# First norm by scaling and transposing, with the loads of tokens and weights in another order, in a one-core hybrid encoder layer

## The chip, the cores and the metric

The kernel runs on one core of a Trainium2 chip. The metric is the device time of one execution in microseconds; the median of the runs is what counts. The engines of the core are TensorE (PE in the profile; its weight loads are PEld), VectorE (DVE), ScalarE (ACT), GpSimd (POOL) and SyncE (SP, which here only issues DMAs).

## What is computed

One layer of an encoder on 512 tokens of 1024 channels, in float32. The first step is an RMS norm; its result `h` goes through one wide projection whose columns feed a recurrent branch (RG-LRU), a gated DeltaNet branch in both directions, and gates. Both branches are projected, gated, added to the tokens; a second norm and a SwiGLU feed-forward follow, then a last norm.

```python
def rmsnorm(x, g):
    y = x * rsqrt(mean(x * x, -1) + EPS)
    return y * g

h = rmsnorm(x, mix_norm)                     # the step that is changed
rx, ry, qkv, z, ba, gates = split(h @ w_in)  # 1024 x 9248
y_rnn = rglru_branch(rx, ry, ...) @ w_rnn_proj
y_dn = deltanet_branch(qkv, z, ba, ...) @ w_dn_proj
x = x + (sigmoid(g_rnn) * y_rnn + sigmoid(g_dn) * y_dn) @ w_out
gt, up = split(rmsnorm(x, ffn_norm) @ w_gate_up)
x = x + (silu(gt) * up) @ w_down
return rmsnorm(x, final_norm)
```

## The kernel before

Nearly all arithmetic is matrix products on TensorE. A float32 operand is split into a high part (rounded to the format fp32r) and a low part (the rest), and a product is the sum of three: high by high, high by low, low by high (`mm3`, L591). A split costs one copy on ScalarE and one subtraction on VectorE.

**The first norm.** Tokens come as four blocks of 128 (`xs`, L505 to L511), each 128 x 1024 with tokens on the partitions. For each block `rms_rstd` (L463) sums the squares, on ScalarE for the first block of a pair and on VectorE for the second, and takes the reciprocal of the root. The projection needs channels on the partitions, so a block has to be transposed. `norm_scale` (L485) multiplies a 128 x 128 identity by the tokens' factors, which gives a diagonal matrix `dg`, and `norm_transpose` (L490) multiplies each 128 x 128 piece of the tokens with it on TensorE: scaling and transposing are one float32 product. Four such products (two pieces of channels, two blocks of tokens) fill one PSUM buffer of the three called `ax`. ScalarE then writes the high part `hh` with the gain as a scale, VectorE the low part `hl` (L502, L503).

**The projection.** A step of the projection takes 128 columns of `w_in`. `weights` (L588, by `stage`, L571) loads them into one of three buffers `wraw` and splits them into `whi` and `wlo`, two buffers each; `in_proj` (L600) multiplies them with `hh` and `hl`, eight pieces of channels, 24 products with 512 tokens. For the first four calls in the program the tokens are taken as two halves of 256 (L604), so 48 products with 256 columns. `rg_front` (L686) is such a step for one of the twelve blocks of the recurrent branch, followed by a convolution and four small gate products, whose weights are loaded to the one buffer `graw` in two DMAs (L692, L693). A narrow step (L620 to L634) projects the 32 columns of `ba`. The second norm (L1230 on) already scales the tokens on VectorE and then transposes the scaled ones with `turn` (L441), TensorE's transpose against the identity.

**The order of the work.** Nothing is issued as it is written. `Rec` (L319) notes every operation with an estimated cost, and `Plan.order` (L144) lays them out: it steps through time, and whenever an engine is free it takes that operation, among those whose inputs are done and whose buffers are free, which has the lowest key. The key is the stage's entry in the table `TIMES` (L35) plus the offset `plan.t` inside the stage; `spend` (L433) begins a new stage. Stages beyond the table (the feed-forward and the end) follow in the order of the program. Costs per engine are in L340 to L372; `TABLES` (L58) says which function tables serve which function of ScalarE, so that the planner can count the loads. SyncE's DMAs are laid out by the same keys. The loads of tokens have the offset -300 (two blocks) and -20 (the other two), weights -40.

In the order before, SyncE issues the four token blocks, then the columns of `ba`, the weights of one step, gate weights, and more weights. TensorE begins with the products on `dg`, and among them runs the `ba` step and then the step of recurrent block 5 with 512 tokens.

Of the kernel before, what the change touches and what calls it, by code (L numbers as in the profile page):

```python
# [53 lines left out]
class Plan:  # L54
# [3 lines left out]
    TABLES = {AF.Exp: ("exp", "lnexp"), AF.Tanh: ("exp", "sigmoid", "silu", "gelu"), AF.Sigmoid: ("sigmoid",), AF.Sqrt: ("sqrt",),  # L58
              AF.Ln: ("lnexp",), AF.Silu: ("silu",), AF.Gelu_apprx_tanh: ("gelu",)}
# [259 lines left out]
class Rec:  # L319
# [5 lines left out]
    def __getattr__(self, op):  # L325
        real = getattr(self.real, op)

        def call(*a, **kw):
# [25 lines left out]
            elif e == "ACT":  # L354
                cost = (51 if psum else 93) + 0.834 * n + 93 * (ptr if n > 1 else len(ins) - 1) + (93 if len(outs) > 1 else 0)
                if op == "activation":
                    table = Plan.TABLES.get(a[2])
# [13 lines left out]
            else:  # L371
                cost = {"tensor_tensor": 150 + 2.1 * n, "memset": 35 + 0.834 * n, "affine_select": 140 + 0.886 * n}.get(op, 240 + 0.84 * n)  # L372
# [6 lines left out]
def trunk(ctx: ExitStack, tc: tile.TileContext, x, mix_norm, w_in, rg_conv_w, rg_conv_b, rg_wa, rg_ba, rg_wx, rg_bx,  # L379
# [42 lines left out]
    def small(shape, tag, bufs=2, dt=F32):  # L422
        return new(sp, shape, tag, bufs, dt)
# [39 lines left out]
    def rms_rstd(src, c):  # L463
        ssq = small([P, 1], "ssq", 4)
        if c % 2:
# [40 lines left out]
    for c in range(NT):  # L506
# [3 lines left out]
        if c == 1:  # L510
            plan.t = -20.0  # L511
# [1064 lines left out]
```

## Time and profile before

| | |
|---|---|
| median of 3 runs | 1075.23 us (1075.0 to 1075.24) |
| the profiled execution | 1074.94 us |
| its span, from the first to the last instruction | 1073.2 us |
| mean granted TensorE clock | 0.998 |
| PE busy | 1052.4 us, 6793 matmuls |
| VectorE busy | 905.1 us |
| ScalarE busy | 665.2 us, of it 67 table loads, 86.0 us |
| DMA | 118.59 MB, mean 111 GB/s |

How to read the rows below: a row of the timeline is start, length (us), engine, line, operation, what is written and read, how many were merged, and in brackets the idle time before it and what ended it. All operations are issued through one helper, so that all have the line L373; one goes by the names of the buffers. A row of groups ends with busy time, mean ns of one, and idle time before. A row of windows begins with the stretch, its length, and then busy time and number of instructions for PE, PEld, DVE, ACT and POOL, the clock, the DMA share and GB/s. A busy PE includes the drain of matmuls that overlap, so that the length of one matmul (0.28 to 0.4 us) is more than the distance to the next.

### The profile page before, as it was taken

The numbers are of one execution on the slowest core, as the hardware profiler recorded it, in microseconds if no ns is written. First come the engines' busy times: TensorE is split into PE (matmuls) and PEld (weight loads), VectorE is DVE, ScalarE is ACT, GpSimd is POOL, SyncE is SP. The second block draws the span as 40 slices with busy tenths as digits, with TensorE's granted clock in tenths as the row PEclk, the third lists the DMA queues.
The fourth block names the chain that finished last, engine by engine and source line by source line (L and its number), as shares of the span: only waits on it lengthen the run. The fifth ranks groups of instructions, "written<-read, shape, count | busy, mean of one in ns | idle before, by whom it ended". The sixth has DMA issues, their size and how long they took to land.

```text
span 1073.2 us, 17710 instructions
## 1 busy us (share of the span) xinstructions
PE 1052.4 (98%) x6793; PEld 915.9 (85%) x6793; DVE 905.1 (84%) x1631; ACT 665.2 (62%) x1191; POOL 44.0 (4%) x93
## 2 busy tenths in 40 slices
PE   7999999999999999999999999999999999999997
PEld 6988887888878887988898888889999999998885
DVE  6669999778986996699669947669999988889997
ACT  6899899795457437655784445357454544446664
POOL 2000000003010101101010000000000000000000
PEclk9999999999999999999999999999999999999999
DMA  7332423223231132122312214455567433425633
GB/s 202 103 89 57 131 79 89 70 74 103 84 90 50 45 108 60 41 79 76 82 40 70 79 47 143 132 181 177 178 218 259 142 99 99 118 80 196 212 135 104
DMA packets 165892, 118.59 MB, mean 111 GB/s; under 512 B 5680, under 2 KB 152224, under 8 KB 165808
## 3 DMA queue, kind: packets, MB, share of 16 engines
q1 hardware_dynamic: 164336, 114.18, 35.6%
q10 hardware_dynamic: 1184, 3.15, 0.8%
q8 instruction: 53, 0.87, 0.3%
q14 instruction: 31, 0.25, 0.1%
q0 software_dynamic: 288, 0.13, 0.1%
HBM read 109.59 MB, written 7.86 MB: 109 GB/s over the span
## 4 chain that ended last, share of the span: by engine, by line
PE 84%; DVE 7%; ACT 5%; DMA 1%; issue 1%; SPq 0%; DVEq 0%; ACTq 0%
PE mm L373 48%; PE ax L373 23%; PE st L373 14%; DVE t L373 5%; ACT t L373 3%; DVE wlo L373 1%; ACT na L373 1%; ACT whi L373 1%; DMA wraw<-in_w_in_dram 1%; DVE na L373 1%; ACT L373 1%; DMA wraw<-in_w_gate_up_dram 0%; ACT ax L373 0%; SPq L373 0%; ACT hh L373 0%
## 5 line engine op out<-in xcount | busy, mean ns | idle before, releaser
L373 DVE TENSOR_TENSOR t<-t,t 128x512 fp32r<-128x512 f32 (+20 forms) x466 | 246.9, 544 | 21.8 <-ACT t L373 14.5
L373 PE MATMUL mm<-hl,whi 128*128 128x512 f32 (+2 forms) x704 | 242.5, 356 | 0.4 <-DVE hl L373 0.4
L373 PE MATMUL mm<-hh,whi 128*128 128x512 f32 (+2 forms) x704 | 241.9, 356 | 0.7 <-ACT whi L373 0.7
L373 ACT CAST whi<-wraw 128x1024 fp32r<-128x1024 f32 (+3 forms) x142 | 133.1, 940 | 161.0 <-PE mm L373 78.1
L373 DVE TENSOR_TENSOR wlo<-wraw,whi 128x1024 fp32r<-128x1024 f32 (+3 forms) x141 | 153.2, 1089 | 58.0 <-ACT whi L373 22.1
L373 PE MATMUL mm<-hh,wlo 128*128 128x512 f32 (+1 forms) x688 | 152.3, 355 | 0.0
L373 PEld LDWEIGHTS mm<-hh,whi 128*128 128x128 f32 (+1 forms) x704 | 132.4, 188 | 18.5 <-ACT whi L373 1.5
L373 PEld LDWEIGHTS mm<-hl,whi 128*128 128x128 f32 (+1 forms) x704 | 132.5, 188 | 18.0 <-DVE hl L373 1.5
L373 PE MATMUL ax<-t,t 32*32 32x32 f32 (+3 forms) x1062 | 139.9, 286 | 3.0 <-ACT t L373 2.8
L373 PEld LDWEIGHTS mm<-hh,wlo 128*128 128x128 f32 x688 | 116.2, 189 | 17.4
L373 PEld LDWEIGHTS ax<-t,t 128*128 128x128 f32 (+1 forms) x1062 | 108.7, 159 | 21.0 <-ACT t L373 6.9
L373 ACT CAST t<-t 128x512 fp32r<-128x512 f32 (+2 forms) x128 | 81.5, 652 | 55.2 <-DVE t L373 50.3
L373 PE MATMUL mm<-t,t 128*128 128x256 f32 (+1 forms) x468 | 90.6, 336 | 0.6 <-DVE t L373 0.6
L373 ACT ACT_TABLE_LOAD x67 | 86.0, 1283 | 4.4 <-PEq L1562 1.7
L373 DVE SCALAR_TENSOR_TENSOR t<-mm,par,t 128x511 f32<-128x511 f32 (+1 forms) x108 | 79.5, 743 | 3.4 <-ACT t L373 2.7
L373 PE MATMUL mm<-t,whi 128*128 128x512 f32 x320 | 82.2, 394 | 0.0
L373 PEld LDWEIGHTS mm<-t,t 128*128 128x128 f32 x468 | 72.7, 190 | 9.6 <-DVE t L373 0.8
L373 PEld LDWEIGHTS mm<-t,whi 128*128 128x128 f32 x320 | 59.2, 188 | 12.1 <-ACT whi L373 0.2
L373 ACT ACTIVATE t<-t 128x128 f32<-128x128 f32 (+4 forms) x84 | 46.1, 559 | 18.9 <-DVE t L373 16.8
L373 ACT CAST t<-wraw 128x1024 fp32r<-128x1024 f32 (+1 forms) x48 | 41.7, 870 | 21.0 <-DMA wraw<-in_w_gate_up_dram 8.3
L373 DVE TENSOR_TENSOR t<-wraw,t 128x1024 fp32r<-128x1024 f32 (+1 forms) x48 | 47.9, 998 | 2.3 <-ACT t L373 2.2
L373 PE MATMUL mm<-t,wlo 128*128 128x512 f32 x160 | 44.6, 396 | 0.0
(212 smaller groups left out, 1672.3 us busy)
## 6 DMA issues: line engine op xcount, KB each, us to landing
wraw<-in_w_in_dram SPq DMA_DIRECT2D x72, 512.0 KB, 3.8
wraw<-in_w_gate_up_dram SPq DMA_DIRECT2D x44, 512.0 KB, 4.1
wraw<-in_w_rnn_proj_dram SPq DMA_DIRECT2D x16, 384.0 KB, 3.5
bg<-in_w_down_dram SPq DMA_DIRECT2D x11, 512.0 KB, 4.6
sums<-bg SPq DMA_DIRECT2D x11, 512.0 KB, 4.7
wraw<-sums SPq DMA_DIRECT2D x11, 512.0 KB, 4.5
wraw<-in_w_down_dram SPq DMA_DIRECT2D x22, 256.0 KB, 2.7
wraw<-in_w_down_dram SPq DMA_DIRECT2D x11, 512.0 KB, 3.6
```

The costliest lines, as they stand in the source:

```text
L373: self.plan.add(e, lambda: real(*a, **kw), outs, ins, cost, tail, table)
```

## The change

1. `norm_scale` and `dg` go. `norm_transpose` scales each block on VectorE into a new 128 x 1024 buffer and transposes the scaled pieces with `turn`.
2. The sum of squares: for the first block of each pair ScalarE takes 512 channels and VectorE the other 512, whose scaled sum enters the root as its bias; for the second block ScalarE takes all 1024.
3. The first pair of token blocks is loaded and normed in one stage, the second pair in a stage of its own, parameters and `ba` in two more. By the keys, SyncE's order becomes: token blocks 0 and 1, the weights of recurrent block 0, its gate weights, the weights of recurrent block 1, token blocks 2 and 3, and then the other weights.
4. Twenty products of the matrix of ones with itself are put ahead of the norm on TensorE; their result is not used.
5. The first three projection steps (recurrent blocks 0, 1, 2) take `weights_k`, which splits into buffers of the large pool (22 buffers) instead of `whi` and `wlo`. `weights_k` and `parts_of` are the same functions as before, moved up from the feed-forward.
6. The gate weights of the first three blocks are loaded with the offset -12 instead of -40.
7. The planner: Exp and Ln no longer share a table, strided copies on ScalarE cost 100 ns more, GpSimd's operations have another price.
8. `TIMES` has new values for all stages up to the second norm (159 entries for 156), so that the order changes there on all engines. In the new table the first steps are recurrent blocks 0 and 1, then block 2, `ba`, and blocks 5, 4 and 3.

The core of the diff, without the numbers of the table:

```diff
-    TABLES = {AF.Exp: ("exp", "lnexp"), ...
-              AF.Ln: ("lnexp",), ...
+    TABLES = {AF.Exp: ("exp",), ...
+              AF.Ln: ("ln",), ...
...
+                if op == "copy" and len(dims) > 2 and dims[-1][1] <= 64:
+                    cost += 100
...
-                cost = {"tensor_tensor": 150 + 2.1 * n, ...}.get(op, 240 + 0.84 * n)
+                cost = {...}.get(op, 240 + 1.2 * n)
...
+    def rms_rstd(src, halves):
+        sa, rst, rin = (small([P, 1], t, 4) for t in ("ssq", "rst", "rin"))
+        n = 512 if halves else D
+        A.activation(four(shape=(P, D))[:, 0:n], src[:, 0:n], AF.Square, accum_out=sa)
+        bias = eps_t
+        if halves:
+            bias = small([P, 1], "ssh", 4)
+            V.scalar_tensor_tensor(two(), src[:, n:D], 1.0, src[:, n:D], ALU.mult, ALU.mult, accum_out=bias)
+            V.tensor_scalar(bias, bias, 1.0 / D, EPS, ALU.mult, ALU.add)
+        act(rst, sa, AF.Sqrt, scale=1.0 / D, bias=bias)
         V.reciprocal(rin, rst)
         return rin
...
-    def norm_scale(src, c):
-        dg = small([P, P], "dg", 4)
-        V.tensor_scalar(dg, ident, rms_rstd(src, c), None, ALU.mult)
-        return dg
...
+        for i, src in enumerate(srcs):
+            t = four(shape=(P, D))
+            V.tensor_scalar(t, src, rms_rstd(src, i == 0), None, ALU.mult)
+            sc.append(t)
...
-                    T.matmul(pt[...], srcs[i][:, kt * P:(kt + 1) * P], dgs[i], start=True, stop=True)
+                    turn(pt[...], sc[i][:, kt * P:(kt + 1) * P])
...
+    for c in range(2):
+        load_x(c)
+    idle = axb()
+    for i in range(20):
+        T.matmul(idle[:, 0:P], ones, ones, start=True, stop=True)
...
+    norm_transpose(xs[0:2], gain, hh, hl, 0)
+    spend()
+    for c in range(2, NT):
+        load_x(c)
+    norm_transpose(xs[2:4], gain, hh, hl, 2)
+    spend()
...
-        hi, lo = weights(win[:, :, col:col + P], KD, P, admit)
+        hi, lo = (weights_k if len(first_tiles) < 3 else weights)(win[:, :, col:col + P], KD, P, admit)
...
-        plan.t = now - 40
+        plan.t = now - (40 if b > 2 else 12)
```

More of the change, by code (lines that the diff above doesn't have):

```diff
@@ L355, in call @@
                 cost = (51 if psum else 93) + 0.834 * n + 93 * (ptr if n > 1 else len(ins) - 1) + (93 if len(outs) > 1 else 0)
+                dims = list(out.ap)
+                if op == "copy" and len(dims) > 2 and dims[-1][1] <= 64:
+                    cost += 100
                 if op == "activation":
@@ L371, in call @@
             else:
-                cost = {"tensor_tensor": 150 + 2.1 * n, "memset": 35 + 0.834 * n, "affine_select": 140 + 0.886 * n}.get(op, 240 + 0.84 * n)
+                cost = {"memset": 35 + 0.834 * n, "affine_select": 140 + 0.886 * n}.get(op, 240 + 1.2 * n)
             self.plan.add(e, lambda: real(*a, **kw), outs, ins, cost, tail, table)
@@ L460, in trunk @@
     V.tensor_copy(sur, su)
-    def rms_rstd(src, c):
-        ssq = small([P, 1], "ssq", 4)
-        if c % 2:
-            V.scalar_tensor_tensor(four(shape=(P, D)), src, 1.0, src, ALU.mult, ALU.mult, accum_out=ssq)
-        else:
-            A.activation(four(shape=(P, D)), src, AF.Square, accum_out=ssq)
-        rst = small([P, 1], "rst", 4)
-        act(rst, ssq, AF.Sqrt, scale=1.0 / D, bias=eps_t)
-        rin = small([P, 1], "rin", 4)
+    def rms_rstd(src, halves):
[8 more added lines that the diff above has]
+        act(rst, sa, AF.Sqrt, scale=1.0 / D, bias=bias)
         V.reciprocal(rin, rst)
@@ L496, in norm_transpose @@
                 for i in range(2):
-                    T.matmul(pt[:, (2 * j + i) * P:(2 * j + i + 1) * P], srcs[i][:, kt * P:(kt + 1) * P], dgs[i], start=True, stop=True)
+                    turn(pt[:, (2 * j + i) * P:(2 * j + i + 1) * P], sc[i][:, kt * P:(kt + 1) * P])
             for j in range(2):
@@ L503, in norm_transpose, with load_x @@
                 V.scalar_tensor_tensor(hl[:, kt, c0 * P:(c0 + 2) * P], pv, gain_[:, kt:kt + 1], f(ho), ALU.mult, ALU.subtract)
-    xs = []
-    for c in range(NT):
-        xc = four(shape=(P, D))
-        Q.dma_start(xc, x[0, c * P:(c + 1) * P, :])
-        xs.append(xc)
-        if c == 1:
-            plan.t = -20.0
-    plan.t = -300.0
+    xs = [four(shape=(P, D)) for _ in range(NT)]
+    def load_x(c):
+        Q.dma_start(xs[c], x[0, c * P:(c + 1) * P, :])
+    for c in range(2):
[3 more added lines that the diff above has]
+        T.matmul(idle[:, 0:P], ones, ones, start=True, stop=True)
     gain = load_gain(mix_norm[0], "gain1")
@@ L515, in trunk @@
     hl = new(hp, (P, KD, S), "hl", 1, F32R)
-    for c0 in (0, 2):
-        norm_transpose(xs[c0:c0 + 2], [norm_scale(xs[c0 + i], i) for i in range(2)], gain, hh, hl, c0)
-        plan.t = -15.0
-    plan.t = 0.0
+    norm_transpose(xs[0:2], gain, hh, hl, 0)
[4 more added lines that the diff above has]
+    spend()
     prow = two(shape=(P, 2, P))
@@ L589, in weights, with parts_of, weights_k @@
         return stage(lambda raw: [(raw[:, :kk, :m], src)], (P, 8, P), lambda t: t[:, :kk, :m], admit)
+    def parts_of(src, hi, lo, ahead):
+        now = plan.t
+        plan.t = now - ahead
+        A.copy(hi, src)
+        V.tensor_tensor(lo, src, f(hi), ALU.subtract)
+        plan.t = now
+    def weights_k(src, *_):
+        now = plan.t
+        raw, hi, lo = new(wp, (P, 8, P), "wraw", NW), four(F32R, (P, 8, P)), four(F32R, (P, 8, P))
+        plan.t = now - 40
+        Q.dma_start(raw, src)
+        plan.t = now
+        parts_of(raw, hi, lo, AHEAD)
+        return hi, lo
     def mm3(po, hi, lo, xh, xl, kk, parts=1):
@@ L1244, in trunk @@
             norm_split(c - 1, a1 if c == 1 else a2)
-    def parts_of(src, hi, lo, ahead):
-        now = plan.t
-        plan.t = now - ahead
-        A.copy(hi, src)
-        V.tensor_tensor(lo, src, f(hi), ALU.subtract)
-        plan.t = now
     wg = w_gate_up[0].rearrange("(k p) n -> p k n", p=P)
@@ L1264, in trunk @@
     BRIDGE = 2
-    def weights_k(src):
-        now = plan.t
-        raw, hi, lo = new(wp, (P, 8, P), "wraw", NW), four(F32R, (P, 8, P)), four(F32R, (P, 8, P))
-        plan.t = now - 40
-        Q.dma_start(raw, src)
-        plan.t = now
-        parts_of(raw, hi, lo, AHEAD)
-        return hi, lo
     def gate_up_plain(n):
```

8 lines of the change are left out of this document (5 added, 3 removed), and 19 rows, old and new, of the table TIMES.

## The prediction

> **What bounds the kernel now.** I read the page first, then the busy time of each engine in long windows, then the waits of TensorE, then the timeline of the first 25 us.
>
> ```profile
> span 1073.2 us, 17710 instructions
> ...
> PE 1052.4 (98%) x6793; PEld 915.9 (85%) x6793; DVE 905.1 (84%) x1631; ACT 665.2 (62%) x1191; POOL 44.0 (4%) x93
> ```
>
> TensorE (PE) is busy for 1052.4 of 1073.2 us, so 20.8 us of idle time is all that it shows. The windows say where that lies.
>
> ```profile
> core 0: us, PE busy (x) PEld busy (x) DVE busy (x) ACT busy (x) POOL busy (x), PEclk, DMA share, GB/s
> ...
> 0.00:12.00 12.00, 5.21 (x26) 4.78 (x26) 5.00 (x16) 5.77 (x13) 6.64 (x21) 1.00 0.90 250
> 12.00:25.00 13.00, 12.56 (x91) 10.48 (x89) 11.25 (x25) 10.34 (x22) 0.00 (x0) 1.00 0.66 169
> 25.00:300.00 275.00, 274.65 (x1305) 227.99 (x1306) 234.83 (x329) 224.23 (x322) 12.29 (x20) 1.00 0.32 89
> 300.00:560.00 260.00, 255.62 (x1973) 215.38 (x1971) 204.26 (x459) 159.40 (x371) 21.93 (x43) 1.00 0.24 67
> 560.00:1050.00 490.00, 489.11 (x3329) 444.46 (x3329) 432.07 (x768) 254.54 (x440) 3.17 (x10) 1.00 0.45 142
> 1050.00:1074.00 24.00, 15.26 (x76) 12.80 (x74) 17.72 (x37) 10.94 (x25) 0.00 (x0) 0.90 0.25 88
> ```
>
> The first two columns after the window are its length and PE's busy time. Idle are 6.8 us in the first 12, 0.4 up to 25, 0.4 up to 300, 4.4 up to 560, 0.9 up to 1050 and 8.7 in the last 24, where results are normed and written. Between 25 and 1050 the waits that have a name are short:
>
> ```profile
> PE ax L373 <- ACT t L373: 2.8, 3, 1.3
> PE ax L373 <- DVE t L373: 1.0, 1, 1.0
> ```
>
> So the kernel is PE's list of work, with a start before it and an end behind it. The change works on the start, and its new table of start times also orders everything up to the second norm. The start, in the SyncE, ScalarE and PE timelines:
>
> ```profile
> 0.80 1.80 SPq L373 DMA_DIRECT2D t<-in_x_dram  x4
> ```
>
> ```profile
> 4.64 1.06 ACT L373 ACTIVATE t<-t 128x1024 f32<-128x1024 f32 x1 [1.40 <-DMA t<-in_x_dram]
> ...
> 5.82 0.29 ACT L373 ACTIVATE rst<-ssq,eps_t 128x1 f32<-128x1 f32 x1
> ...
> 10.80 0.41 ACT L373 CAST whi<-wraw 128x256 fp32r<-128x256 f32 x1 [1.31 <-DMA wraw<-in_w_in_dram]
> 11.12 0.83 ACT L373 ACTIVATE hh<-ax,gain 128x256 fp32r<-128x256 f32 x2
> ```
>
> ```profile
> 6.69 1.65 PE L373 MATMUL ax<-dg,t 128*128 128x128 f32 x6 [3.39 <-DVE dg L373]
> 8.68 3.33 PE L373 MATMUL ax<-dg,t 128*128 128x128 f32 x18 [0.34 <-DVE dg L373]
> 11.82 0.30 PE L373 MATMUL mm<-hh,whi 128*64 128x256 f32 x1
> ```
>
> The four token blocks are issued from 0.80 us. ScalarE waits for the first until 4.64, squares it in 1.06, and the square root starts at 5.82; PE begins its six passes at 6.69 and waits for the second block's scale until 8.68. ScalarE then stands 1.31 us for a DMA of weights (10.80) before it evicts the first transposed rows (11.12); the first product runs at 11.82. VectorE's scale and a later run of passes:
>
> ```profile
> 6.35 0.29 DVE L373 TENSOR_SCALAR dg<-ident,rin 128x128 f32<-128x128 f32 x1
> ...
> 14.71 1.90 PE L373 MATMUL ax<-dg,t 128*128 128x128 f32 x14
> ```
>
> **How much the start costs now.** I count by 24.5 us what PE has given to products:
>
> ```profile
> L373 PE MATMUL ax<-dg,t 128*128 128x128 f32 x64 | 10.3, 319 | 3.8 <-DVE dg L373 3.7
> L373 PE MATMUL mm<-hl,whi 128*64 128x256 f32 x16 | 4.6, 310 | 0.4 <-DVE hl L373 0.4
> L373 PE MATMUL mm<-hh,whi 128*64 128x256 f32 x16 | 4.2, 285 | 0.0
> L373 PE MATMUL mm<-hh,whi 128*128 128x512 f32 x6 | 2.4, 393 | 0.0
> L373 PE MATMUL mm<-hl,whi 128*128 128x512 f32 x5 | 2.0, 392 | 0.0
> ```
>
> The 64 passes on dg are the 32 transposing products with a diagonal: each is two passes. The products are 32 with 256 columns and 11 with 512. What one costs when PE is full, I take from the chain that ended last:
>
> ```profile
> 464.13 16.37 PE mm L373 x72
> ...
> 762.07 2.88 PE mm L373 x24
> ```
>
> 16.37/72 = 0.227 us with 512 columns, 2.88/24 = 0.120 with 256. That is 32 x 0.120 + 11 x 0.227 = 6.3 us of products by 24.5 us; 18.2 us went to the start.
>
> **The change, part by part.** Transposing: a transpose takes one pass where the product with a diagonal takes two:
>
> ```profile
> 210.76 1.25 PE L373 MATMUL ax<-ident,t 128*128 128x128 f32 x10
> ```
>
> Ten take 1.25 us with the last one's drain; less a drain of about 0.2 that is 0.11 each, against 1.90/14 = 0.136 for a pass on dg. The 32 cost PE 3.5 us instead of 64 x 0.12 = 7.7. Of these the first 16 lie in the wait for data; the other 16, 1.8 us, stand among products. The Trainium skill, "TensorE: Matmul & The Clock Gate", section Terms, calls transpose mode four times faster for FP32; by that the second 16 would cost 16 x 0.24 / 4 = 1.0 us, 0.8 less, but the rows here show a factor of two and I go by them.
>
> **Loads.** SyncE now issues the first two token blocks, the weights of recurrent block 0, its two gate weights, the weights of block 1, and only then the other two token blocks; the keys in the table put block 1 ahead of the tokens by 0.1 of its units of time. Rates:
>
> ```profile
> 3.00:6.00 3.00, 0.24 (x1) 0.18 (x1) 0.17 (x1) 1.56 (x5) 2.99 (x7) 1.00 1.01 355
> ...
> 13.00:15.50 2.50, 2.50 (x20) 2.36 (x21) 2.46 (x7) 2.50 (x6) 0.00 (x0) 1.00 1.21 290
> ```
>
> Tokens move at 355 GB/s, weights at 290. A 512 KB token block is then 1.5 us and a weight block 1.8. From 4.64 for the first block I estimate the second at 6.1, weights 0 at 7.9, its gates at 8.8, weights 1 at 10.6, token blocks 2 and 3 at 12.1 and 13.6.
>
> **Norm of the first half.** The chain of one block was 6.35 - 4.64 = 1.71 us from the square to VectorE's scale. The scale now covers the whole block rather than the 128-column diagonal:
>
> ```profile
> L373 DVE TENSOR_SCALAR t<-na,rin 128x1024 f32<-128x1024 f32 x4 | 3.0, 747 | 0.0
> ```
>
> That is 0.75 against 0.29 us, four times: 1.9 us more on VectorE. Block 1 lands at 6.1, is scaled from 7.8 to 8.6; two transposes with their drain end at 9.0. From the first eviction to the first product were 0.7 us (11.12 to 11.82), so the first product runs at 9.8 instead of 11.82. Splitting the first block's square over ScalarE and VectorE takes it off the path, which is block 1's. It adds a wait: the square root of block 0 stands on ScalarE until VectorE's half is summed, and behind it is block 1's square, whose data land at 6.1 only; block 0's half takes about 0.6 us from 4.64, so that wait costs nothing, and would cost its length if VectorE came after 6.1. The wait for weights at 10.80 should go, since weights 0 land at 7.9, and what is late next is block 1's scale.
>
> **The 20 idle products.** They need only the matrix of ones, which GpSimd writes at 0.83:
>
> ```profile
> 0.83 0.20 POOL L373 MEMSET ones<- 128x128 f32 x1
> ```
>
> So they run from about 1.2 us. Forty passes at the early rate, at most 1.65/6 = 0.275, would end at 12.2; at the later 0.136 they end at 6.6. The rate changes between, so about 8.5, beside the wait for the data; in order before the transposes, they delay them by between nothing and 12.2 - 8.6 = 3.6 us; I take nothing, since the path itself arrives at 8.6, and keep the far end for the range.
>
> **From 9.8 us to the second half.** Block 3 lands at 13.6; 1.71 + 0.75 + 0.4 + 0.7 gives its first product at 17.2, a microsecond later if ScalarE is still busy. Until then PE has the halves of blocks 0 and 1, 24 products each, 2.9 us each, the halves of block 2 once it is cast, and transposes. What can keep them back is the preparing:
>
> ```profile
> L373 DVE SCALAR_TENSOR_TENSOR hl<-ax,gain,hh 128x256 fp32r<-128x256 f32 x16 | 6.7, 477 | 1.2 <-ACT hh L373 1.1
> ...
> L373 DVE TENSOR_TENSOR wlo<-wraw,whi 128x1024 fp32r<-128x1024 f32 x2 | 2.4, 1222 | 0.6 <-ACT whi L373 0.6
> ```
>
> ```profile
> L373 ACT ACTIVATE hh<-ax,gain 128x256 fp32r<-128x256 f32 x16 | 6.4, 481 | 0.9 <-PE ax L373 0.9
> ...
> L373 ACT CAST whi<-wraw 128x1024 fp32r<-128x1024 f32 x2 | 2.1, 1062 | 0.8 <-PE mm L373 0.8
> ...
> L373 ACT CAST t<-graw 128x512 fp32r<-128x512 f32 x2 | 1.3, 640 | 0.0
> ```
>
> VectorE has 16 x 0.48 for the low parts, 4 x 0.75 for scales, about 1.2 for two half squares and 0.7 for the gates (by width from the 1.22 row, estimates), 3 x 1.22 for weights, about 1 for small ones: 17.3 us, from 5.0, so to about 22.4. ScalarE has 16 x 0.48, 4 x 0.29, 3.2 of squares, 3 x 1.06 and 0.64: 15.9 us, to 20.5. If PE does the halves of three blocks (8.6 us) and 2.0 of transposes by 22.4, it idles 22.4 - 9.8 - 8.6 - 2.0 = 2.0 us. The bounds are none (the second half's rows are used as they come, from 17.2) and 4.9 (only two blocks are ready).
>
> **The sum.** The start takes 9.8 + 2.0 + 2.0 = 13.8 us instead of 18.2: 4.4 less, between 6.4 (no idle time) and 1.5.
>
> **The other lists of the plan.** The planner now counts separate tables for Exp and Ln, another price on GpSimd and on strided copies of ScalarE, and has a new table of times. After the start the instructions are the same; their order between 25 and about 650 us is not. Nothing in the trace shows the new order. From below, it can gain the 4.4 us of 300:560; from above, a chain can lose its cover. I take 0.1 lost: the named waits are few, and as few can be expected. The weights of the first three blocks go to the pool of 22 wide buffers instead of two; I cost that at nothing, since it frees the two buffers and those 22 are hardly in use then; if a wide tile has to wait, one cast of 1.06 us shows. The end is untouched: 0.
>
> Profiled, 1074.94 - 4.3 = 1070.6 us (its span 1073.2 plus 1.7 around it). The median shown is 1075.23, 0.3 above that run, so I say **1070.9**.
>
> **The rivals.** Starved start: ScalarE and VectorE are the limit; only two blocks' halves are ready and PE idles 4.9 us: a gain of 1.5, 1073.7. For it: VectorE gets 1.9 us more and is busy for 11.25 of 13 us between 12 and 25. Against it: its work of that window doesn't have to end before products go on.
>
> **The order also closes the gaps of the middle.** The 4.4 us between 300 and 560 go too: 1066.5. For it: these waits are for ScalarE and VectorE chains that a planner with better prices can start earlier. Against: no row shows that it does.
>
> **A chain without cover (slower).** The inverse of a head pair ends in a long VectorE transpose and ScalarE copies before PE can go on:
>
> ```profile
> 313.12 2.25 DVE t L373
> ...
> 320.74 1.02 PE ax L373 x63
> ```
>
> From 313.12 to 320.74 are 7.6 us in which PE lives on other products; all of 300:560 lost only 4.4. In the new table the last pair's inverse and state stand behind most gates, with fewer products left to lay beside them. If none is left, 7.6 us are lost, less 4.3: 1078.5. It decides from 4.3 us of uncovered chain on. Against it: the eight output projections of the first six heads are left, 8 x 18 x 0.227 = 33 us, if the third pair is ready by then.
>
> **The clock.** Passes at 6.69 take 0.275 us and those at 14.71 0.136: PE starts at half rate. The 24 early passes took 1.65 + 3.33 us where 24 x 0.136 = 3.3 would do: 1.7 us lost. If transposes and a gap before the products send the rate back, that is lost among products, once or twice: about 1073.4. The Trainium skill, "TensorE: Matmul & The Clock Gate", Part 1 and Part 4, says that the clock opens after about 3.4 us of activity, closes after as long without, and that transpose mode does not count as activity. The two rates agree with the first; on the last the ten transposes at 210.76 say nothing, since they stand between products.
>
> **How the numbers follow.** About 0.2% (2.15 us) is what a measurement tells from no change here. Forecast 0.52 (own range 1068.8 to 1073.7, from the bounds of the start), starved 0.13, better middle 0.15, uncovered chain 0.14, clock 0.06. Faster by over 0.2% is below 1073.1: nearly all of the forecast (0.49), the better middle, and a third of starved and clock: 0.70. Slower is the chain alone, 0.14; the same is what is left, 0.16. Range 1065.5 to 1078.0, which takes in the 3.6 us of the idle products and leaves out what lies beyond the better middle and the chain's full price.
>
> **What would show it.** Right: forty passes on ones before 9 us; 32 single transposes at 0.11; no ScalarE wait for weights at 10 us; the first product near 9.8, and by 24.5 us some 10.7 us of products; PE idle in 25 to 1050 near 5 us; the end as it was. Wrong: the first product after 11, PE idle over 4 us between 10 and 22, transposes at 0.22, or more than 8 us idle between 25 and 1050. If the start measures as said and the time does not, the order of the middle is the step that failed.

## The result, and the profile after

The changed kernel takes 1068.49 us, the median of six runs (1067.69 to 1069.83); the kernel before, on the same chip, takes 1075.24 us (1074.92 to 1076.53, six runs). The ratio is 0.9936, with a 95% interval of 0.9923 to 0.9949: faster by 6.75 us where 4.3 were forecast. The time lies in the stated range of 1065.5 to 1078.0, and 0.3 us below the forecast's own of 1068.8 to 1073.7. The terms that make it up do not lie where I put them.

The page of the kernel after, first its span and then the busy time of the engines (the profiled execution took 1069.83 us, the longest of the six):

```profile
span 1068.1 us, 17717 instructions
...
PE 1053.1 (99%) x6801; PEld 918.5 (86%) x6801; DVE 904.1 (85%) x1633; ACT 670.0 (63%) x1198; POOL 43.2 (4%) x93
```

TensorE still has 1053 us of work, and 15.0 us of the span are idle instead of 20.8. The windows of the kernel after, in the columns and with the bounds of the prediction:

```profile
0.00:12.00 12.00, 8.39 (x45) 7.95 (x46) 3.67 (x12) 4.98 (x10) 6.63 (x21) 1.00 0.91 266
12.00:25.00 13.00, 12.24 (x96) 11.48 (x97) 12.27 (x28) 11.99 (x26) 0.00 (x0) 1.00 0.64 177
25.00:300.00 275.00, 274.67 (x1298) 227.57 (x1297) 240.40 (x344) 222.74 (x324) 9.51 (x22) 1.00 0.32 90
300.00:560.00 260.00, 258.80 (x1992) 219.33 (x1992) 207.56 (x471) 166.30 (x380) 27.08 (x50) 1.00 0.23 63
560.00:1050.00 490.00, 488.83 (x3325) 443.68 (x3324) 427.46 (x752) 254.75 (x437) 0.00 (x0) 1.00 0.46 143
```

In 300:560, where 4.4 us were idle before, 1.2 are left. The first window looks better too (8.39 busy instead of 5.21), but most of that is the forty passes on ones, which are no work.

Idle time alone doesn't say how far a kernel has come, so I use one more measure, worked out from the traces: the **lead**. Each matmul of the list counts with a fixed price (0.227 us with 512 columns, 0.120 with 256 as in the prediction; 0.11 with 128 or fewer, 0.04 for a 64 x 64 and 0.01 for a 32 x 32 product, from their spacing), without the passes on ones and `dg` and the transposes of the first norm. The lead is by how much earlier than the profile of before a profile has reached the same sum. In us, a minus where it is behind; the first column is the run's time, the last the difference of the spans. Counted from the starts or from the ends of matmuls, single entries change by up to 0.6 us at 10 and by 0.3 further on; the differences between two versions of the kernel after change by 0.2 at most, those to e8 by 0.4.

| kernel | median us | at 10 | at 150 | at 290 | at 400 | at 640 | at 900 | end |
|---|---|---|---|---|---|---|---|---|
| after | 1068.49 | 1.3 | 0.8 | 1.9 | 6.3 | 6.9 | 6.3 | 5.1 |
| after, second profile (e11) | 1068.49 | 0.5 | 0.0 | 1.2 | 5.7 | 6.2 | 6.4 | 6.4 |
| e1_gain_early | 1067.03 | 4.1 | 3.7 | 4.7 | 9.1 | 9.7 | 9.0 | 7.9 |
| the same again (e12) | 1065.73 | 4.4 | 3.9 | 5.0 | 9.5 | 10.1 | 10.1 | 9.9 |
| e2_few_idle | 1068.90 | 3.5 | 3.0 | 4.1 | 7.8 | 8.3 | 6.6 | 6.6 |
| e6_tokens_first | 1069.96 | -0.4 | -0.8 | 0.3 | 4.7 | 5.2 | 4.9 | 5.0 |
| e3_after_old_copy | 1075.69 | 1.5 | -2.0 | -0.6 | 1.6 | -1.7 | -1.3 | -1.4 |
| e4_before_copy | 1075.73 | 0.6 | 0.6 | 0.6 | 0.2 | -1.2 | -0.6 | -0.7 |
| e7_after_old_table | 1093.81 | 1.9 | 1.3 | -14.2 | -12.3 | -17.7 | -17.7 | -18.9 |
| e8_after_dg | 1077.62 | 1.2 | -9.4 | -8.0 | -3.5 | -2.7 | -3.3 | -3.4 |
| e5_products_first | 1077.85 | 0.0 | 0.1 | 0.0 | -2.7 | -2.4 | -2.3 | -2.9 |
| e9_neg_early | 1075.37 | 0.1 | 0.2 | 0.2 | -0.3 | -0.1 | 0.0 | -0.6 |
| e10_neg_late | 1069.23 | 2.2 | 1.7 | 2.8 | 5.9 | 6.5 | 6.2 | 6.1 |

The first row shows where the gain lies: the start, where I expected 4.4 us, gives 1.3; the stretch between 290 and 640 us of products, where I expected a tenth of a microsecond lost, gives 5.0; the feed-forward of this one profile gives 1.8 back, which the second profile of the same kernel doesn't.

**Why the start gives so little** stands in the timeline of the kernel after:

```profile
1.09 7.59 PE L377 MATMUL ax<-ones 128*128 128x128 f32 x40 [1.09 <-POOL ones L377]
...
8.61 0.22 PE L377 MATMUL ax<-ident,gain1r 8*128 8x8 f32 x1
...
8.87 0.17 DVE L377 COPY gain<-ax 128x8 f32<-128x8 f32 x1 [3.59 <-PE ax L377]
8.95 0.14 DVE L377 TENSOR_SCALAR ssh<-ssh 128x1 f32<-128x1 f32 x1
9.20 0.29 ACT L377 ACTIVATE rst<-ssq,ssh 128x1 f32<-128x1 f32 x1 [3.89 <-DVE ssh L377]
9.40 1.04 ACT L377 ACTIVATE t<-t 128x1024 f32<-128x1024 f32 x1
...
11.90 1.21 PE L377 MATMUL ax<-ident,t 128*128 128x128 f32 x9 [0.82 <-DVE t L377]
...
13.02 0.38 PE L377 MATMUL mm<-hh,t 128*128 128x256 f32 x1
```

The idle products end at 8.68, as estimated (8.5). But behind them in TensorE's order stands the transpose of the gain, a 128 x 8 tile that nobody needs before 10 us (8.61). VectorE's copy of it waits 3.59 us, and VectorE too works in order: behind the copy stands the half sum of squares `ssh` of token block 0 (8.95). ScalarE's root of block 0 waits for that half sum for 3.89 us (9.20), and behind the root stands the square of block 1 (9.40), whose data had landed by then: with the gain moved, in e1 below, the same square runs at 5.71. The first product runs at 13.02, later than the 11.82 of before. What is still won lies behind it: transposes at one pass each, and products that come without gaps.

**Where the middle gains** I read from the first inverse of a head pair. Timelines of TensorE, before and then after:

```profile
317.35 0.74 PE L373 MATMUL ax<-t,na 32*32 32x32 f32 x64 [0.97 <-DVE t L373]
318.02 1.43 PE L373 MATMUL mm<-hh,wlo 128*128 128x512 f32 x5
320.74 1.02 PE L373 MATMUL ax<-t,t 32*32 32x32 f32 x96 [1.29 <-ACT t L373]
```

```profile
313.75 0.75 PE L377 MATMUL ax<-t,na 32*32 32x32 f32 x64
314.44 1.42 PE L377 MATMUL mm<-hh,wlo 128*128 128x512 f32 x5
315.79 1.02 PE L377 MATMUL ax<-t,t 32*32 32x32 f32 x96
```

Before, the two groups of 32 x 32 products wait 0.97 and 1.29 us; after, for nothing. In the second wait PE stands for `t<-ax`, the negated copy of the first group's result. ScalarE's timelines, before and then after, show what is ahead of that copy:

```profile
317.89 0.83 ACT L373 CAST whi<-wraw 128x768 fp32r<-128x768 f32 x1
318.63 0.82 ACT L373 COPY t<-t 32x256 f32<-32x256 f32 x2
319.46 0.82 ACT L373 COPY na<-t 32x256 f32<-32x256 f32 x2
320.30 0.38 ACT L373 ACTIVATE t<-ax 128x256 f32<-128x256 f32 x1
```

```profile
313.77 0.82 ACT L377 COPY t<-t 32x256 f32<-32x256 f32 x2
314.60 0.40 ACT L377 COPY na<-t 32x256 f32<-32x256 f32 x1
314.91 0.37 ACT L377 ACTIVATE t<-ax 128x256 f32<-128x256 f32 x1
315.31 1.23 ACT L377 COPY na<-t 32x256 f32<-32x256 f32 x3
```

The first group's result is there 0.7 us after its start. Before, that is at 318.09, and four block copies, 1.6 us, then stand ahead of the negated copy, behind a cast of weights; after, it is at 314.50, with one block copy ahead (314.60), and three follow. A block copy takes 0.41 us, and the 100 ns that the change adds to the planner's prices are for copies of this form. The second head pair has the same waits before (1.96 us of idle time in 370:430, against 0.71 after). Of the lead of 5.0 us, 3.5 lie in the steps from a wide product to a group of 32 x 32 products, summed over the nine such steps between 290 and 640; the rest is spread over the spacing of the other products.

### The profile page after: what moved, and what is told of

Its sections match the earlier page's. It is cut to its first block, busy times and chain, and to the rows that moved or that the text cites. A ratio compares the mean times of both kernels' runs of the same rounds, so it can differ in the third digit from the quotient of the medians.

```text
span 1068.1 us, 17717 instructions
## 1 busy us (share of the span) xinstructions
PE 1053.1 (99%) x6801; PEld 918.5 (86%) x6801; DVE 904.1 (85%) x1633; ACT 670.0 (63%) x1198; POOL 43.2 (4%) x93
## 4 chain that ended last, share of the span: by engine, by line
PE 75%; DVE 12%; ACT 8%; issue 2%; DMA 2%; SPq 0%; ACTq 0%; DVEq 0%; POOL 0%; POOLq 0%
PE mm L377 43%; PE ax L377 21%; PE st L377 12%; DVE t L377 9%; ACT t L377 4%; DVE wlo L377 2%; ACT L377 1%; ACT whi L377 1%; DVE na L377 1%; DMA wraw<-sums 1%; DMA wraw<-in_w_gate_up_dram 1%; ACT na L377 0%; DMA wraw<-in_w_down_dram 0%; ACT hh L377 0%; DVE hh L377 0%
## 5 line engine op out<-in xcount | busy, mean ns | idle before, releaser
L377 DVE TENSOR_TENSOR t<-t,t 128x512 fp32r<-128x512 f32 (+18 forms) x466 | 246.1, 541 | 22.5 <-ACT t L377 15.0
L377 PE MATMUL mm<-hl,whi 128*128 128x512 f32 (+2 forms) x656 | 229.4, 360 | 0.0
L377 PE MATMUL mm<-hh,whi 128*128 128x512 f32 (+2 forms) x656 | 228.6, 359 | 0.0
L377 DVE TENSOR_TENSOR wlo<-wraw,whi 128x1024 fp32r<-128x1024 f32 (+3 forms) x138 | 150.1, 1087 | 68.5 <-ACT whi L377 38.6
L377 PE MATMUL mm<-hh,wlo 128*128 128x512 f32 (+1 forms) x640 | 147.2, 361 | 0.0
L377 PEld LDWEIGHTS mm<-hh,whi 128*128 128x128 f32 (+1 forms) x656 | 123.2, 188 | 17.4 <-ACT whi L377 0.4
L377 PEld LDWEIGHTS mm<-hl,whi 128*128 128x128 f32 (+1 forms) x656 | 123.2, 188 | 17.1
L377 PEld LDWEIGHTS mm<-hh,wlo 128*128 128x128 f32 x640 | 109.4, 189 | 17.0
L377 ACT ACTIVATE t<-t 128x128 f32<-128x128 f32 (+4 forms) x86 | 47.3, 561 | 24.0 <-DVE t L377 21.6
L377 ACT CAST t<-wraw 128x1024 fp32r<-128x1024 f32 (+1 forms) x51 | 45.0, 884 | 22.4 <-DMA wraw<-in_w_gate_up_dram 6.3
L377 DVE TENSOR_TENSOR t<-wraw,t 128x1024 fp32r<-128x1024 f32 (+1 forms) x51 | 51.7, 1014 | 1.5 <-ACT t L377 1.3
```

The costliest lines, as they stand in the source:

```text
L377: self.plan.add(e, lambda: real(*a, **kw), outs, ins, cost, tail, table)
```

## The experiments

The theory after the profile of the changed kernel had two parts. **Start:** the gain's transpose behind the idle products holds up the norm; rivals were that the norm is late by its own chain, that the clock does it, or the loads. **Middle:** the planner's price for small copies puts the inverse's copies right; rivals were that the table does it, that the norm's new steps do it, or that it is the place of a few instructions that could be moved by hand.

### The start

**e1_gain_early**: the kernel after, but TensorE's transpose of the gain stands behind the sixth idle product instead of the twentieth; all else in the same order.

```diff
         todo = plan.order()
+        todo.remove(turn0)                           # the gain's transpose
+        todo.insert(todo.index(idle0 + 6), turn0)
```

> The kernel after with one instruction moved: TensorE's transpose of the gain stands behind the sixth of the 20 idle products, instead of behind the last; every other order is kept. Theory (in-order blocking: idle products -> gain's transpose -> VectorE's copy of the gain -> the half sum behind it -> ScalarE's root and block 1's square): the copy of the gain comes near 4 us instead of 8.87, the root of block 0 near 5.7 instead of 9.20, the first product near 10 instead of 13.02, and the time is 2 to 3 us lower than the kernel after, 1065.5 to 1066.5. Rival (the second half of the tokens sets the start): the first product comes early too, but TensorE then idles as long before the second half; the time stays within 0.7 of the kernel after.

It took 1067.03 us (1065.09 to 1067.51), ratio 0.9919 (0.9906 to 0.9933), 1.46 below the median of after and so less than the 2 to 3 us expected; side by side on one chip (e11 and e12 below) the two kernels differ by 2.76. Its timeline, all engines:

```profile
4.93 0.16 DVE L377 COPY gain<-ax 128x8 f32<-128x8 f32 x1
...
5.30 0.29 ACT L377 ACTIVATE rst<-ssq,ssh 128x1 f32<-128x1 f32 x1 [0.27 <-DVE ssh L377]
...
5.71 1.06 ACT L377 ACTIVATE t<-t 128x1024 f32<-128x1024 f32 x1
...
7.42 0.75 DVE L377 TENSOR_SCALAR t<-t,rin 128x1024 f32<-128x1024 f32 x1
7.65 1.05 ACT L377 CAST t<-wraw 128x1024 fp32r<-128x1024 f32 x1 [0.46 <-DMA wraw<-in_w_in_dram]
...
8.96 0.62 ACT L377 CAST t<-graw 128x512 fp32r<-128x512 f32 x1 [0.26 <-DMA graw<-in_rg_wx_dram]
9.65 2.30 ACT L377 ACTIVATE hh<-ax,gain 128x256 fp32r<-128x256 f32 x6
...
10.18 0.38 PE L377 MATMUL mm<-hh,t 128*128 128x256 f32 x1
```

One instruction of 0.2 us, moved, brings the root from 9.20 to 5.30, block 1's square from 9.40 to 5.71 and the first product from 13.02 to 10.18. The lead over before is 4.1 at 10 us of products, and the 2.8 us more than after's hold through every column to the end. The theory of the start stands. What comes last in front of the first product is now ScalarE: block 1 is scaled from 7.42 to 8.17, but ScalarE casts the weights and the gates first and evicts the first transposed rows at 9.65.

**e2_few_idle**: the same, with the last fourteen of the twenty idle products left out (their result is not used).

```diff
+        gone = set(range(idle0 + 6, idle0 + 20))
+        todo = [i for i in todo if i not in gone]
```

> The kernel after with 6 idle products instead of 20, else the same order. Theory: the gain is free near 4 us as in the run before, but the transposes and first products run at the early half rate, so of the 2 to 3 us up to 1.7 is given back: 1066 to 1067.5. Rival (the idle products pay for themselves, the warm clock is what the start needs): slower than the kernel after, 1069 or more.

1068.90 us (1068.28 to 1069.63), ratio 0.9942 (0.9930 to 0.9955): 1.9 above e1 on the same chip, more than the 1066 to 1067.5 that the theory gave and just under its rival's 1069. PE's timeline and a window of its profile:

```profile
8.25 2.18 PE L377 MATMUL ax<-ident,t 128*128 128x128 f32 x9 [0.98 <-DVE t L377]
10.10 0.58 PE L377 MATMUL mm<-hh,t 128*128 128x256 f32 x1
```

```profile
8.00:16.00 8.00, 7.45 (x39) 7.09 (x40) 6.71 (x14) 7.59 (x16) 0.54 (x1) 0.59 1.13 289
```

The first product comes at 10.10, as early as in e1, but the clock granted in 8:16 is 0.59 (by the trace's clock record it is at half rate from 7.67 to 14.49), nine transposes take 2.18 us and a product 0.58 instead of 0.38. So the idle products do pay for themselves, with 0.6 us at the start. The distance to e1 then grows, to 1.4 us at 640 and 2.4 at 900, and is 1.3 at the end of the profiles; I have no cause for that later part. Fewer idle products are no better way.

**e6_tokens_first**: e1 with token blocks 2 and 3 loaded ahead of all weights, as in the kernel before.

```diff
+        todo = [i for i in todo if i not in loads[2:]]
+        k = todo.index(loads[1]) + 1
+        todo[k:k] = loads[2:]
```

> The kernel of the first experiment (gain early) with token blocks 2 and 3 loaded right behind 0 and 1 again, ahead of all weights; all other orders kept. Theory (the order of loads brings the first weights while the first half is normed): weights 0 land about 3 us later, near 10.7, ScalarE waits for them ahead of its first evictions, the first product comes near 12.5 instead of 10.18 and the time rises by 1 to 2.5, to 1068 to 1069.5. Rival (the loads don't matter, their time lies beside the norm): within 0.7 of 1067.0.

1069.96 us (1069.49 to 1072.38), ratio 0.9953 (0.9940 to 0.9965), 2.9 above e1, which ran on another chip, where the kernel before took 0.4 us less. The waits of TensorE have a new row, and a window shows the clock behind it:

```profile
PE mm L377 <- ACT hh L377: 3.7, 1, 3.7
```

```profile
16.00:24.00 8.00, 8.00 (x58) 8.00 (x57) 7.01 (x16) 5.99 (x14) 0.00 (x0) 0.80 0.38 108
```

The first product runs at 13.30. ScalarE stands 4.11 us for the weights, until 11.32, with the first evictions behind it, PE waits 3.7 us for them, and then the clock is at half rate from 12.38 to 19.21. The start loses 4.5 us. So the order of the loads is a part of the change that works, worth more than I expected.

**e11_after_again, e12_gain_early_again**: the kernel after and e1 once more, without another edit, side by side on one chip.

> The kernel after, unchanged, for a comparison on the same chip in the same job: 1068.5 within 0.8.

> The first experiment (the gain's transpose behind the sixth idle product), unchanged, beside the kernel after in the same job. By the profiles its start is 2.85 us shorter; the medians had 1.5. If the start's gain reaches the end: 2 to 3 us below the kernel after of this job. Rival (the feed-forward waits for its weights and takes part of it back): 1 to 1.6 below.

1068.49 us (1067.50 to 1068.62), ratio 0.9934 (0.9922 to 0.9947), and 1065.73 us (1065.01 to 1067.33), ratio 0.9913 (0.9899 to 0.9926): the early gain is worth 2.76 us here; between the two profiles it is 3.9 us at the start and 3.5 at the end. It is the fastest version found, faster than both kernels. The second profile of after also shows something that its first did not. Windows of e11 and then of e12:

```profile
12.00:25.00 13.00, 12.69 (x82) 12.29 (x81) 10.63 (x26) 10.60 (x24) 0.00 (x0) 0.74 0.69 189
```

```profile
12.00:25.00 13.00, 12.74 (x106) 12.41 (x105) 12.46 (x28) 10.92 (x23) 0.00 (x0) 1.00 0.93 229
```

In e11 the forty passes end 0.9 us earlier, and the first product runs at 12.09 instead of 13.02; yet the lead at 10 us is 0.8 smaller, since the clock is at half rate from 12.01 to 18.84. That is 1.7 us lost. The gap that the late gain leaves in front of the first products can so cost the clock: one profile of after keeps its rate, this one and that of e10 (0.88 in 12:25) lose it, both profiles with the early gain keep it.

### The middle

**e3_after_old_copy** takes the price on ScalarE's strided copies out of the kernel after, **e4_before_copy** adds it to the kernel before.

```diff
-                dims = list(out.ap)
-                if op == "copy" and len(dims) > 2 and dims[-1][1] <= 64:
-                    cost += 100
```

> The kernel after without the planner's 100 ns on ScalarE's strided copies; table and all else kept, so the order is laid out anew. Theory (the middle was won by that price: the inverse's ScalarE copies take 0.4 us where the plan of before says 0.3, so TensorE stood in front of them): the TensorE idle time of some 2 us at each of the first two inverses is back, 1071 to 1073. Rival (the new table of times won it): within 1 us of the kernel after.

> The kernel before with the 100 ns on ScalarE's strided copies and nothing else of the change. Theory of the price: TensorE idles about 1 us instead of 4.4 between 300 and 560, 1071 to 1072.5. Rival of the table: 1074.5 to 1076.

1075.69 us (1073.71 to 1076.90, 11 runs), ratio 1.0001 (0.9992 to 1.0010), and 1075.73 us (1074.57 to 1078.18, 11 runs), ratio 1.0011 (1.0002 to 1.0019): both within 0.2% of before. e4 came as its rival said; e3 lost more than its theory gave (1071 to 1073). One window of e3 and one of e4:

```profile
300.00:560.00 260.00, 255.12 (x1971) 214.66 (x1970) 199.66 (x452) 164.07 (x369) 22.88 (x46) 1.00 0.23 65
```

```profile
300.00:560.00 260.00, 254.72 (x1963) 215.26 (x1962) 202.35 (x451) 154.37 (x360) 21.41 (x40) 0.99 0.23 65
```

Without the price, waits of the middle are back (4.9 us idle) and 3.5 us more are lost between 10 and 150 us of products. Those 3.5 us are one wait for a cast of weights, and the clock behind it, which is at half rate for 3.41 us (from 156.63 to 160.04):

```profile
156.04 0.50 PE L374 MATMUL mm<-hh,whi 128*128 128x512 f32 x1 [1.82 <-ACT whi L374]
```

But the price alone doesn't take the waits of the middle away (5.3 idle in e4). "The price does it" falls. Whether the price itself is needed with something else is not shown: in e3 the new table meets prices that it did not come with, and the order changes from the first weights on. The planner's other two price changes, for Exp and Ln and for GpSimd, were not run alone.

**e7_after_old_table**: the kernel after, with the table of before from the stages behind the first projection steps on.

```diff
-TIMES = ta
+TIMES = ta[:7] + tb[4:]        # ta: the table of after, tb: that of before
```

> The kernel after with the table of before for all stages from the first recurrent gates on; the first seven entries (norm, loads, parameters, blocks 0 to 2) and the planner's new prices stay. Theory (start and middle are separate gains, the middle is the table's): the start gains its 1.3 us, the middle nothing: 1073 to 1075. Rival (the new norm and loads bring it all): 1068 to 1070.

1093.81 us (1092.21 to 1095.10), ratio 1.0170 (1.0156 to 1.0183). That is far outside both expectations. The start keeps its lead of 1.9, and 16 us are lost by 290. The window of that stretch:

```profile
25.00:300.00 275.00, 264.06 (x1223) 215.99 (x1222) 222.11 (x301) 222.27 (x320) 10.21 (x20) 0.98 0.30 83
```

A table that made 274.65 busy of 275 with the norm and the prices that it came with leaves 11 us idle with others, and the clock is at half rate for 13.7 us of that stretch besides. This run so doesn't tell whose the gain of the middle is.

**e8_after_dg**: the norm of before (diagonal products, no idle products) in the kernel after; loads, prices and table stay.

```diff
-            t = four(shape=(P, D))
-            V.tensor_scalar(t, src, rms_rstd(src, i == 0), None, ALU.mult)
+    dgs = [norm_scale(xs[i], i) for i in range(2)]    # and products with dg, as before
-    idle = axb()                                      # and its twenty products
```

> The kernel after with the norm of before: diagonal products and the old sums of squares, no idle products; loads, table and prices kept. The gain's transpose then waits for nothing. Against the first experiment (1067.0), theory (a transpose costs one pass instead of two): 16 x 0.12 us of the second half's passes stand among products and the first half's passes run at the early half rate of 0.21 us, so the start loses 2 to 4 us to the first experiment: 1069 to 1071. Rival (the way of transposing doesn't matter, only the loads' order does): 1067 within 0.7.

1077.62 us (1076.18 to 1078.52, 10 runs), ratio 1.0020 (1.0011 to 1.0030). Two windows:

```profile
25.00:300.00 275.00, 268.41 (x1257) 221.60 (x1256) 231.07 (x327) 213.64 (x315) 10.82 (x22) 0.99 0.29 82
300.00:560.00 260.00, 258.80 (x1992) 219.24 (x1991) 207.21 (x466) 163.37 (x372) 27.07 (x50) 1.00 0.24 67
```

The time lies outside both expectations. Up to 150 us of products the order that the same table gives to other instructions loses 10.6 us: in 25:300 the named waits sum to 6.6 us, and the clock is at half rate for 6.83 us (from 156.55). From 290 on it does what it does in after: 258.80 busy, to the digit, and 5.3 us of lead between 290 and 640. So the gain of the middle doesn't need the new norm. It doesn't need the new order of the token loads either: e6, without it, gains 4.9 us there. What is left is the table and the prices together (and the buffers and load times of the first three weights, which no run put back). The norm's own share can't be read from this total, because its loss is that of a plan laid anew; at 10 us of products the old norm leads before by 1.2 where e1 leads by 4.1.

**e5_products_first** and **e9_neg_early** are the kernel before with one thing moved by hand. In e5, TensorE's order gets products that are ready ahead of the two waiting groups of the first inverse (by the trace four ahead of the first and five ahead of the second); in e9, ScalarE's negated copy stands ahead of four block copies at the first two inverses. **e10_neg_late** is the reverse of e9 in the kernel after: the negated copy behind three more block copies.

```diff
+        for r in negs[:2]:              # e9; in e10 the three behind r go ahead of it
+            acts = [i for i in todo if plan.ops[i][0] == "ACT"]
+            n = acts.index(r)
+            back = acts[n - 4:n]
+            todo = [i for i in todo if i not in back]
+            n = todo.index(r) + 1
+            todo[n:n] = back
```

> The kernel before with one thing moved on TensorE alone: at the first head pair's inverse, four products stand ahead of the first group of small products and six ahead of the second (they stood behind them); all other engines keep their order. Theory (in the middle TensorE stood in its own order before small products whose ScalarE copies were late, with ready products behind them): the waits of 0.97 and 1.29 us there go, TensorE's idle time in 300 to 560 falls from 4.4 to about 2.2 and the time by about 2, to 1072.5 to 1073.5. Rival (the inverse's chain itself sets the time there): the waits come back within the same pair and the time stays, 1074.5 to 1075.7.

> The kernel before with one ScalarE operation moved at each of the first two inverses: the negated copy that releases the second group of small products stands ahead of four block copies instead of behind them; all other engines keep their order. Theory (ScalarE's order at the inverse sets the middle: of 320.30 the copy comes to 318.7): TensorE's wait of 1.29 us for it at the first pair goes and as much time is saved behind that pair, at the second pair perhaps half, since a weights cast is late there next: 1.3 to 2 us in the profile's work by then, 1073.3 to 1074.3. Rival (what is saved is lost later in the same inverse, as in the run with products moved): no gain behind the first pair, 1075 or more.

> The kernel after with the reverse: at the first two inverses the negated copy stands behind three more block copies (1.23 us). Theory: TensorE waits up to 1.2 us more at each, 1 to 2.4 us in all: 1069.5 to 1071. Rival (the order of TensorE's products, not ScalarE's, made the middle): within 0.7 of the kernel after of this job.

e5 took 1077.85 us (1074.76 to 1080.26, 11 runs), ratio 1.0019 (1.0010 to 1.0029), slower rather than faster. TensorE's timeline and a window:

```profile
320.67 1.26 PE L373 MATMUL ax<-t,t 32*32 32x32 f32 x96 [0.95 <-ACT t L373]
323.04 0.44 PE L373 MATMUL ax<-t,na 64*64 64x64 f32 x2 [1.10 <-ACT t L373]
...
324.42 0.63 PE L373 MATMUL mm<-hl,whi 128*128 128x512 f32 x1
```

```profile
320.00:330.00 10.00, 8.19 (x142) 6.18 (x144) 4.14 (x6) 4.73 (x12) 0.00 (x0) 0.66 0.34 93
```

The chain runs on ScalarE: products that are used up ahead of it are missing behind it, the wait of 1.29 becomes 0.95 and 1.10, and then the clock falls (0.66; a product takes 0.63 instead of 0.39). By the clock record the rate is halved from 322.60 to 329.43, which costs up to 3.4 us and is more than the 2.7 lost. Of the eleven executions, the two whose mean clock was 0.998 took 1074.76 and 1075.32, no more than the kernel before on that chip (1075.51): without the fall of the clock the move costs nothing and wins next to nothing. My theory that PE's order of products is what the change mends is not borne out.

e9 took 1075.37 us (1074.08 to 1077.39, 11 runs), ratio 1.0002 (0.9993 to 1.0011). Its negated copy is early (318.40 instead of 320.30), and the group behind it starts at 319.15 instead of 320.74; TensorE's timeline at the first inverse:

```profile
319.15 0.74 PE L373 MATMUL ax<-t,t 32*32 32x32 f32 x62
320.57 0.43 PE L373 MATMUL ax<-t,t 32*32 32x32 f32 x34 [0.68 <-issue]
```

The second half of the group stands until 320.57. What was won is lost inside the same inverse, but for 0.2 us, and at the second inverse another wait comes, of 1.78 us for weights, with the clock at half rate behind it (from 422.52 to 425.94). e10 took 1069.23 us (1068.84 to 1069.57), ratio 0.9944 (0.9931 to 0.9958), 0.74 above after on the same chip, between what its theory (1 to 2.4) and its rival (within 0.7) gave. TensorE's timeline at its first inverse:

```profile
315.76 1.02 PE L377 MATMUL ax<-t,t 32*32 32x32 f32 x96 [0.85 <-ACT t L377]
```

With 1.36 us at the second inverse the waits are back, and from 290 to 400 us of products its lead grows by 3.1 where that of after grows by 4.4 to 4.5. So ScalarE's order at these two inverses is worth 1.3 to 1.4 of the 5 us. Which of the other decisions of the plan make the rest stays open: e9 says that this one alone brings nothing to the kernel before, the fall of the clock at the second inverse included.

## Why the prediction was right, and where not

The sign came out, and the size came out by luck: an error of one sign at the start and one of the other sign in the middle nearly cancel. One of the prediction's own signs of being wrong did appear: the first product came after 11, at 13.02.

**What bounds the kernel**: held. PE's busy time is the same within 0.7 us, since the passes on ones (busy for 7.6 us) and the 32 transposes (4.9) take the place of the passes on `dg` (10.3), and what changed is idle time and what it is busy with.

**The start, 13.8 us instead of 18.2.** By the same count (24.5 us less the products done by then) after measures 16.3 us, and before 18.1. The term that failed is that of the idle products, of which I wrote "I take nothing, since the path itself arrives at 8.6". I had looked at what they delay on TensorE, and not at the one instruction between them and the transposes that feeds VectorE. With the gain early the same count gives 14.2 us (e1) and 14.0 (e12). So the other terms came out in size: the first product at 10.18 and 9.93 (9.8 forecast), weights 0 at 7.65 (7.9 forecast), no wait for weights at 10 us, and behind the first product 1.8 us without work up to 24.5 (2.0 forecast). The transposes cost 0.11 (nine take 1.21 us with their drain), half of the two passes of before. The Trainium skill's page "TensorE: Matmul & The Clock Gate", Terms, calls transpose mode four times faster for FP32; the runs show a factor of two. But "what is late next is block 1's scale" was wrong: in e1 the scale is done at 8.17, and ScalarE's casts of weights and gates hold the first eviction until 9.65; that the product came near 9.8 all the same is luck. Two sums of the prediction are off without moving the forecast: its idle times add up to 21.6 us instead of 20.8, since the last window reaches beyond the span, and 17.3 us of VectorE from 5.0 end at 22.3. Of the half sum on VectorE I had written that the wait "would cost its length if VectorE came after 6.1". It came at 8.95, for a reason that I hadn't looked for.

**The loads**: right in what they do, and e6 gives them a price that I hadn't worked out, 4.5 us at the start and 2.9 in the median.

**The middle, 0.1 lost**: wrong; the rival "the order also closes the gaps of the middle" happened, at 3.2 us of idle time in 300:560 of the 4.4, and 5.0 of lead. I had said that no row shows the new order; that is true, but the price of 100 ns named the instructions, and the rows of before had them at 0.41 us each and ahead of the copy that PE waited for. There was so some evidence for that rival, and I weighed it at 0.15. Added to the forecast's own start the rival would have been 1066.5; what kept the time above that is the start, and with the early gain the medians lie on both sides of it (1067.03 and 1065.73).

**Starved start**: not so. VectorE is busy for 12.27 of 13 us in 12:25, but products go on: between the first product (13.02) and 24.5, less the 8.2 us of products and 14 transposes at 0.11, 1.7 us are left idle, not 4.9.

**The uncovered chain**: not so; in the profile of after no wait between 300 and 560 is longer than 0.7 us. Under a table that isn't its own the same kernel loses 25 us against after (e7), but 16 of them ahead of 290 us of products.

**The clock**: the rival's mechanism does occur, at a price of 1.7 us, in the second profile of after and not in the first. The Trainium skill ("TensorE: Matmul & The Clock Gate", Parts 1 and 4) says that the clock opens and closes after about 3.4 us, counted in a free-running window, and that a transpose doesn't count as a busy PE in the same way. The runs agree with the window: inside the kernels, the stretches at half rate in the clock records last 3.41, 6.83 or 10.24 us, so the rate changes at the ends of windows of 3.41 us. With the late gain 4.3 us lie between the last pass on ones and the first product, and where the windows lie decides. In e11 the clock opens at 5.19; the window from 8.60 to 12.01 holds twelve transposes and no product, and the rate falls at 12.01. In the first profile of after it opens at 7.12; the window from 10.53 to 13.95 holds eleven transposes and two products, and the rate stays. With six idle products (6.1 us, e2) and with late weights (5.1 us, e6) it falls; with the early gain (2.2 us or less) it doesn't. Of the eleven executions of after, only the one first profiled has a mean clock of 0.999; the others have 0.995 to 0.997, so that the fall may be the rule. Yet that one is the longest of them.

That transposes count for nothing the runs don't show, and they speak against it. I add up what the matmuls in each window cost at the prices of the lead, a transpose at 0.11. The 26 windows of the 14 traces after which the clock closes hold at most 1.51 us (twelve of them lie inside the kernels, the others at their ends); the 4301 after which it stays open hold at least 1.44. Without the transposes that order breaks: in e3 a window with one product, 0.12 us, and twelve transposes stays open, while windows with 0.6 to 1.5 us of products alone close. So not a single gap closes the clock, but a window with less than about 1.4 to 1.5 us of work in 3.41; the figure is mine, worked out from these traces.

**The end, 0**: right for the norm and the output: from the start of the last products to the end of the span it is 9.2 us in both profiles. Between 640 us of products and the end the lead of the first profile falls by 1.8 and that of the second grows by 0.2, in the same order of instructions; what makes the feed-forward vary so, by waits for DMAs of weights, stays open.

## What to carry to other kernels

Filler on an engine that works in order is free only if nothing small is queued behind it: follow each consumer of what comes next, through the in-order queues of the other engines, before a filler is costed at nothing. A written-out table of start times goes with one list of instructions and one set of prices; changing any of the three alone cost between 7 and 25 us here, and a price alone brought nothing. To find where a change gains, compare the time at which two profiles have done the same products, not the idle time by windows alone.

## What the runs showed of the hardware

The granted clock also falls in the middle of a full kernel. In e5, small products (32 x 32 and 64 x 64) with waits of 0.95 and 1.10 us among them were enough: PE was busy for 8.19 of 10 us in 320:330 and the clock was 0.66, with 128 x 512 products at 0.63 us instead of 0.39. No single wait there is near the 3.4 us without activity at which, by the Trainium skill ("TensorE: Matmul & The Clock Gate", Part 1), the clock closes. The same groups in before, with waits of 0.97 and 1.29 us, kept 1.00. By the count above, the window of e5 that ends at 322.60, where the rate falls, holds 1.19 us of work (one wide product and 96 of 32 x 32, which count 0.01 each), and the one of before from 318.11 to 321.53 holds 1.84. A wait at such a place can so cost more than its length.

The forty passes of the idle products took 7.59, 6.67 and 6.52 us in three profiles of after and e10, from the same start: by the clock records the clock opens at 7.12, 5.19 and 4.86, so that the moment differs by over 2 us between executions. Ahead of the first record the clock column of the windows reads 1.00, as in 0:12, also where passes run at half rate (twelve on ones in 2.93 us in e12, the other twenty-eight in 3.61).
